# Scores of both softmax maps as alternating 64-row matmuls, drains on VectorE, and a head's Newton steps on GpSimd

## The chip, the core and the metric

The kernel runs on one core of a Trainium2 chip. The metric is the device time of one execution in microseconds (us). The engines of the core are TensorE (PE in the rows, its weight loads PEld), VectorE (DVE), ScalarE (ACT), GpSimd (POOL) and the DMA queue of SyncE (SP). Each works through its own list of instructions in order, and they wait for each other by semaphores.

## What is computed

One layer of a mixer: a projection feeds a differential attention (8 heads, two softmax maps per head) and a recurrent branch, and both go through one output projection. The part that the change touches is the attention with the output projection around it. Cut from the reference:

```python
def one_block(qblk):                                   # 128 queries
    s = jnp.einsum('bqhmd,bkhmd->bhmqk', qblk, k) * scale   # m: two maps, d = 64
    p = jax.nn.softmax(s, axis=-1)
    a = p[:, :, 0] - lam * p[:, :, 1]
    return jnp.einsum('bhqk,bkhe->bqhe', a, v)
o = diff_attention(q, k_all, v_all, lam)
att = (rms_norm(o, g_subln) * (1.0 - lam_init)) * jax.nn.silu(g_att)
...
out = jnp.concatenate([att, lru], axis=-1) @ w_out
x_new = x + gate * rms_norm(out, g_post)
```

There are 128 context and 1024 latent tokens. A block of context queries sees 128 keys, a block of latent queries 1152 (1024 latent and 128 cached).

## The kernel before, in words

To keep close to float32, every product is made of three matmuls: each operand is split into a high part in a rounded float32 and a low part that holds the rest, and high x high, high x low and low x high are added (`mm3`, L117 to L119).

Up to some 430 us the kernel normalises the input and works on the recurrent branch; from 430 to 730 us it projects queries, keys and values and stores them in DRAM (`qk_block`, `v_block`; per head `qs`, `ks`). Then comes the attention loop, up to some 1225 us, and after it the rest of the output projection and the final normalisation.

The loop has 72 tiles: 8 heads by 9 blocks of 128 queries. The block of context queries is a small tile of 128 keys; it stands first in each head but the last, and last in the last. `period(n)` emits the work of tile n, and the order of emission is the order on each engine. For a tile and a map:

- `scores(n, mp)` makes the scores in one of two PSUM buffers of three banks (tag `big`), 3 x 384 columns. Before, the high part of the query stands twice in its tile, in rows 0 to 63 and 64 to 127, and the key tile of a map holds the high and the low part of the keys one above the other. So one matmul of 128 rows (L1076) gives high x high and high x low at once, and one of 64 rows (L1078) adds low x high.
- VectorE takes the maximum (L1085) and corrects that of map 0 by a constant (L1088), ScalarE the exponential with its sum (L1092).
- `recip` and `combine` make the factor (L1100, L1102) and e1 x factor - e0 (L1111) of the tile before; ScalarE casts it to float16 (L1114), GpSimd makes the float16 remainder (L1115), and SP transposes both by DMA (L1117).
- `pv(n - 4)` multiplies the transposed weights of the tile four periods back with the values (27 matmuls of 128 columns), ScalarE copies the result to `ot` and squares it.

The buffers of the exponentials (`e0`, `e1`) and of the casts (`a16`) are two deep each.

Between these the loop does most of the output projection: a granule is three matmuls of 512 columns (`out_mm`), four granules fill a unit in the PSUM bank `po`, and a unit is drained into `acc` in SBUF (`out_evac`): the first 18 by a ScalarE copy, the next by a ScalarE copy to `ev` (L1039) and an add on GpSimd (L1040), the last few by VectorE (L1042). `GRANULES` lists for each period how many granules stand after map 0's scores and how many after map 1's.

When a head is done, `mean_squares` and `root` compute 1 / sqrt of its mean squares by Newton steps on 9 columns. Before, these wait in the list `tiny`, and `fill()` puts one behind each of the loop's VectorE instructions. Then `scale` multiplies the head's output on GpSimd (L1161), TensorE transposes it into the spare columns of score buffers (L1165), and VectorE multiplies in the gate (L1169).

## Time and profile before

| what | us |
|---|---|
| median of three runs (1293.74 to 1298.01) | 1294.49 |
| the profiled execution | 1297.48 |
| its span, first to last instruction | 1295.1 |
| TensorE / VectorE busy in the span | 1220.8 / 968.3 |
| ScalarE / GpSimd busy in the span | 680.1 / 479.1 |

How to read the rows below: a row of the timeline gives the start in the span, the length, the engine, the line, the operation and what it writes and reads; `x3` means three of one kind merged. Matmuls overlap in their pipeline, so the distance from one start to the next says what one costs, not its length. In brackets stands the idle time of the engine before the row and what ended it.

### The profile page before, as it was taken

How to read it: one execution, taken by the hardware profiler on the slowest of the kernel's cores; microseconds unless marked ns; L12 is line 12 of the kernel's file. 1: busy time of each engine (PE TensorE's matmuls, PEld its weight loads, DVE VectorE, ACT ScalarE, POOL GpSimd, SP SyncE). 2: the span in 40 equal slices, each digit the busy share in tenths (PEclk: the TensorE clock that was granted, in tenths of full speed). 3: DMA queues.
4: the chain of work that ended last, by engine and by line, in shares of the span. 5: the costliest groups of instructions: out<-in, count | busy, mean ns of one | idle time of the engine just before them, and what ended most of it. 6: DMA issues, size and time to landing. Idle time of an engine off the chain costs nothing.

```text
span 1295.1 us, 19733 instructions
## 1 busy us (share of the span) xinstructions
PE 1220.8 (94%) x7672; PEld 1069.4 (83%) x7672; DVE 968.3 (75%) x1253; ACT 680.1 (53%) x1152; POOL 479.1 (37%) x244
## 2 busy tenths in 40 slices
PE   6899999999999899999999699999999989999887
PEld 1499999999999899989999577776777766777666
DVE  4938779777979828666473257888898989899977
ACT  4446545654665233332232357677667676766632
POOL 0421112111212334424242214346655566555624
PEclk9999999999999899999999899999999998999999
DMA  9221222123212757446272659899899988899864
GB/s 364 103 72 41 91 93 93 60 74 111 76 54 102 214 165 220 151 161 167 88 218 68 228 127 201 193 214 249 174 214 224 226 218 191 201 207 217 205 202 167
DMA packets 262916, 208.62 MB, mean 161 GB/s; under 512 B 158876, under 2 KB 228252, under 8 KB 262056
## 3 DMA queue, kind: packets, MB, share of 16 engines
q1 hardware_dynamic: 262536, 206.52, 59.0%
q8 instruction: 60, 0.98, 0.3%
q10 hardware_dynamic: 288, 0.85, 0.2%
q14 instruction: 32, 0.26, 0.1%
HBM read 112.16 MB, written 56.90 MB: 131 GB/s over the span
## 4 chain that ended last, share of the span: by engine, by line
PE 67%; DVE 20%; issue 4%; DMA 4%; ACT 3%; SPq 1%; POOL 1%; DVEq 0%; ACTq 0%; POOLq 0%
PE s L1078 5%; DVE mx L1085 4%; PE s L1076 4%; PE po L117 3%; DVE e L1111 3%; PE ga L119 3%; PE ga L117 3%; PE ga L118 3%; PE po L119 3%; PE po L118 3%; PE v L118 2%; PE v L117 2%; PE v L119 2%; PE x L118 2%; PE x L119 2%
## 5 line engine op out<-in xcount | busy, mean ns | idle before, releaser
L114 POOL TENSOR_TENSOR wlo<-wraw,whi 128x1024 fp32r<-128x1024 f32 x48 | 129.5, 2698 | 421.6 <-ACT whi L262 418.0
L1115 POOL TENSOR_TENSOR a<-e,a 128x1152 f16<-128x1152 f32 (+1 forms) x72 | 156.0, 2166 | 212.3 <-ACT a L1114 210.3
L1085 DVE TENSOR_REDUCE mx<-s 128x1 f32<-128x1152 f32 (+1 forms) x144 | 176.8, 1233 | 65.8 <-PE s L1078 64.1
L1092 ACT ACTIVATE e<-s,mx 128x1152 f32<-128x1152 f32 (+1 forms) x144 | 162.4, 1128 | 77.0 <-DVE fa L1100 29.7
L1111 DVE SCALAR_TENSOR_TENSOR e<-e,fa,e 128x1152 f32<-128x1152 f32 (+1 forms) x72 | 119.0, 1653 | 6.7 <-DVE fa L1102 0.5
L1076 PE MATMUL s<-kt,qt 128*128 128x384 f32 (+1 forms) x400 | 100.3, 355 | 19.5 <-ACT e L1092 18.0
L117 PE MATMUL po<-woh,lt 128*128 128x512 f32 x216 | 97.2, 450 | 16.3 <-ACT e L1092 13.9
L1114 ACT CAST a<-e 128x1152 f16<-128x1152 f32 (+1 forms) x72 | 76.0, 1055 | 60.8 <-DVE e L1111 52.7
L1078 PE MATMUL s<-kt,qt 64*128 64x384 f32 (+1 forms) x400 | 107.0, 369 | 0.0
L117 PE MATMUL pv<-vt,t 128*128 128x128 f16 x584 | 103.5, 222 | 1.9 <-ACT ot L1130 1.9
L118 PE MATMUL pv<-vt,t 128*128 128x128 f16 x584 | 102.8, 220 | 0.0
L119 PE MATMUL pv<-vt,t 128*128 128x128 f16 x584 | 102.8, 220 | 0.0
L1076 PEld LDWEIGHTS s<-kt,qt 128*128 128x128 f32 x400 | 69.1, 192 | 31.8 <-ACT e L1092 24.3
L1078 PEld LDWEIGHTS s<-kt,qt 64*128 64x128 f32 x400 | 63.7, 187 | 34.8 <-issue 34.2
L119 PE MATMUL po<-woh,lt 128*128 128x512 f32 x216 | 86.7, 401 | 0.0
L118 PE MATMUL po<-wol,lt 128*128 128x512 f32 x216 | 86.6, 401 | 0.0
L117 PE MATMUL v<-whi,hTh 128*128 128x256 f32 x288 | 81.8, 284 | 0.0
L119 PE MATMUL v<-whi,hTl 128*128 128x256 f32 x288 | 81.5, 283 | 0.0
L118 PE MATMUL v<-wlo,hTh 128*128 128x256 f32 x288 | 81.5, 283 | 0.0
L117 PEld LDWEIGHTS po<-woh,lt 128*128 128x128 f32 x216 | 41.4, 192 | 41.1 <-issue 15.9
L117 PEld LDWEIGHTS <-t 128*128 128x128 f16 x584 | 57.5, 98 | 17.7 <-issue 17.5
L117 PE MATMUL k<-hTh,whi 128*128 128x384 f32 x192 | 66.4, 346 | 4.8 <-ACT qfk L633 4.8
(299 smaller groups left out, 3588.0 us busy)
## 6 DMA issues: line engine op xcount, KB each, us to landing
wraw<-in_w_in_dram SPq DMA_DIRECT2D x48, 512.0 KB, 3.5
qt<-qs SPq DMA_DIRECT2D x72, 192.0 KB, 3.6
lt<-mix SPq DMA_DIRECT2D x27, 512.0 KB, 4.6
kt<-ks SPq DMA_DIRECT2D x16, 640.0 KB, 6.2
qs<-hiq SPq DMA_DIRECT2D x32, 288.0 KB, 5.8
wa<-in_w_ada_dram SPq DMA_DIRECT2D x16, 512.0 KB, 10.9
wor<-in_w_out_dram SPq DMA_DIRECT2D x32, 256.0 KB, 3.3
mix<-amo SPq DMA_DIRECT2D x6, 1152.0 KB
```

Source lines behind the costliest of these rows:

```text
L114: eng.tensor_tensor(out=lo, in0=val, in1=f(hi), op=ALU.subtract)
L117: PE.matmul(out, lhsT=lh, rhs=rh, start=start, stop=False)
L118: PE.matmul(out, lhsT=lh, rhs=rl, start=False, stop=False)
L119: PE.matmul(out, lhsT=ll, rhs=rh, start=False, stop=stop)
L1076: PE.matmul(sps[:, j, :w_], lhsT=qt[:, mp], rhs=kt_[:, mp, c], start=True, stop=False)
L1078: PE.matmul(sps[:, j, :w_], lhsT=qt[rows, 2], rhs=kt_[rows, mp, c], start=False, stop=True)
L1085: V.tensor_reduce(out=d["mx"][:, mp:mp + 1], in_=sv, axis=AX.XY, op=ALU.max, negate=True)
L1092: S.activation(out=e_[:, :nk].rearrange("p (j c) -> p j c", c=w_), in_=sv, func=AF.Exp, bias=d["mx"][:, mp:mp + 1], accum_out=total)
L1111: V.scalar_tensor_tensor(out=e1, in0=e1, scalar=d["fa"], in1=e0, op0=ALU.mult, op1=ALU.subtract)
L1114: S.copy(out=a16[:, 0:nk], in_=e1)
L1115: G.tensor_tensor(out=a16[:, nk:2 * nk], in0=e1, in1=a16[:, 0:nk], op=ALU.subtract)
```

## The change

**Scores.** `scores(n)` now scores both maps of a tile in one go. The query is stored once, its high and low part as two tiles with map 0 in rows 0 to 63 and map 1 in rows 64 to 127, and so are the keys. Each of the three products is a matmul of 64 rows, and map 0 and map 1 take turns. On TensorE, before, around the second map of a tile (`s_1` is its score buffer, `kt` and `qt` keys and query, `po` the output projection):

```order
L119 MATMUL pv_8435<-vt_7449,t_25_8240 128x128
L1076 MATMUL s_1_8475<-kt_7925,qt_2_8185 128x384 [waits Activation_49]
L1076 MATMUL s_1_8475<-kt_7925,qt_2_8185 128x384 x2
L1078 MATMUL s_1_8475<-kt_7925,qt_2_8185 128x384 x3
L117 MATMUL po_1_1_8413<-woh_1_8094,lt_1_7776 128x512
```

and now, at a tile's start (`s_0` and `s_1` are the buffers of its two maps):

```order
L99 MATMUL po_0_1_8432<-wol_1_8283,lt_0_7761 128x512 [waits Pool_49]
L100 MATMUL po_0_1_8432<-woh_1_8282,lt_0_7761 128x512
L1038 MATMUL s_0_8535<-kt_8028,qt_2_8286 128x384 [waits DMAHW6_49,Activation_49]
L1038 MATMUL s_1_8536<-kt_8028,qt_2_8286 128x384 [waits Activation_49]
L1038 MATMUL s_0_8535<-kt_8028,qt_2_8286 128x384
```

Eighteen matmuls of two maps stand together, and the first two wait for one exponential each; value product and granules follow behind them, no longer between the maps.

**Softmax, drains and factor.** `softmax(n, mp)` holds what followed the scores. Both maxima of a tile come before the drain and the combination of the tile before. Every unit is drained by VectorE. The factor is a scalar instruction instead of a tensor one. On VectorE, before (maxima `mx`, factor `fa`, exponentials `e`):

```order
L1102 SCALAR_TENSOR_TENSOR fa_8466<-fa_8466,lam,kq_8269 128x1 [waits DVE_49]
L1111 SCALAR_TENSOR_TENSOR e_1_8411<-e_1_8411,fa_8466,e_0_8361 128x1152 [waits DVE_49,Pool_49]
L1085 TENSOR_REDUCE mx_8422<-s_1_8475 128x1 [waits PE_49]
L1085 TENSOR_REDUCE mx_8499<-s_0_8501 128x1 [waits PE_49]
L1088 TENSOR_SCALAR mx_8499<-mx_8499,lsig 128x1 [waits DVE_49]
L1100 RECIPROCAL fa_8543<-sm_8423 128x1 [waits Activation_49]
```

and now:

```order
L1050 TENSOR_REDUCE mx_8533<-s_0_8535 128x1 [waits PE_49]
L1053 TENSOR_SCALAR mx_8533<-mx_8533,lsig 128x1 [waits DVE_49]
L1050 TENSOR_REDUCE mx_8533<-s_1_8536 128x1 [waits PE_49]
L1004 TENSOR_TENSOR acc_6236<-acc_6236,po_1_1_8593 128x512 [waits PE_49]
L1067 RECIPROCAL fa_8607<-sm_8454 128x1 [waits Activation_49]
L1069 TENSOR_SCALAR fa_8607<-fa_8607,lam,kq_8381 128x1 [waits DVE_49]
L1077 SCALAR_TENSOR_TENSOR e_1_8480<-e_1_8480,fa_8607,e_0_8477 128x1152 [waits DVE_49,Pool_49]
```

The combination of the tile before moved from ahead of the second maximum to behind it, and a drain (L1004) stands between.

**Granules.** The list holds one number per period, 4 or 2 (8 in period 3); they stand behind `pv`.

**Newton steps.** `apart(h, 0)` puts four small instructions on GpSimd at the end of period b + 8 (b is the head's first period plus 4), `apart(h, 1)` two on VectorE and twelve on GpSimd at the end of b + 9, with `scale` behind them. This holds for seven heads; the last keeps its way. On GpSimd, before (`a` remainder of a tile, `acc` output sums, `ot` head output):

```order
L1115 TENSOR_TENSOR a_30_8614<-e_1_8560,a_30_8614 128x1152 [waits DMAHW1_49,Activation_49]
L1040 TENSOR_TENSOR acc_6280<-acc_6280,ev_0_8656 128x512 [waits Activation_49]
L1115 TENSOR_TENSOR a_31_8702<-e_1_8628,a_31_8702 128x1152 [waits DMAHW5_49,Activation_49]
L1161 TENSOR_TENSOR ot_7888<-ot_7888,y_7885 128x1152 [waits DVE_49]
L1115 TENSOR_TENSOR a_32_8779<-e_1_8716,a_32_8779 128x1152 [waits DMAHW0_49,Activation_49]
```

and now, up to the first of three equal rounds of four, and the end:

```order
L1121 TENSOR_TENSOR xc_7973<-xc_7973,tt_7972 128x9 [waits Pool_49]
L1081 TENSOR_TENSOR a_30_8754<-e_1_8648,a_30_8754 128x1152 [waits DMAHW7_49,Activation_49]
L1126 TENSOR_TENSOR tt_7972<-y_7971 128x9 [waits DVE_49,Pool_49]
L1127 TENSOR_TENSOR tt_7972<-tt_7972,xc_7973 128x9 [waits Pool_49]
L1128 TENSOR_SCALAR tt_7972<-tt_7972 128x9 [waits Pool_49]
L1129 TENSOR_TENSOR y_7971<-tt_7972,y_7971 128x9 [waits Pool_49]
...
L1146 TENSOR_TENSOR ot_7974<-ot_7974,y_7971 128x1152 [waits Pool_49]
L1081 TENSOR_TENSOR a_31_8858<-e_1_8730,a_31_8858 128x1152 [waits DMAHW3_49,Activation_49]
```

The adds of the output sums left GpSimd; the Newton steps stand between two remainders. The core of the diff:

```diff
-    qs = [dr.tile([P, 3, T], F32R, name=f"qs{h}") for h in range(NH)]
+    qs = [dr.tile([P, 2, T], F32R, name=f"qs{h}") for h in range(NH)]
...
             def send():
-                hi, lo = d["hl"]
-                if which == 0:
-                    for m2 in range(2):
-                        for r in (slice(0, 64), slice(64, 128)):
-                            move(out=qs[h][r, m2], in_=hi[64 * m2:64 * m2 + 64])
-                    move(out=qs[h][:, 2], in_=lo)
-                else:
-                    for mp in range(2):
-                        for part, val in enumerate((hi, lo)):
-                            r = 64 * (mp ^ part)
-                            move(out=ks[r:r + 64, mp, h, 0:T], in_=val[64 * mp:64 * mp + 64])
+                for part, val in enumerate(d["hl"]):
+                    move(out=ks[:, part, h, 0:T] if which else qs[h][:, part], in_=val)
...
             if first:
-                S.copy(out=dst, in_=po)
-            elif shared and turns["i"] % EVERY == 0:
-                ev = op.tile([P, 512], F32, tag="ev", name=f"ev{t}_{half}")
-                S.copy(out=ev, in_=po)
-                G.tensor_tensor(out=dst, in0=dst, in1=ev, op=ALU.add)
+                V.tensor_copy(out=dst, in_=po)
             else:
                 V.tensor_tensor(out=dst, in0=dst, in1=po, op=ALU.add)
...
-            for j, c in enumerate(cols):
-                PE.matmul(sps[:, j, :w_], lhsT=qt[:, mp], rhs=kt_[:, mp, c], start=True, stop=False)
-            for j, c in enumerate(cols):
-                PE.matmul(sps[:, j, :w_], lhsT=qt[rows, 2], rhs=kt_[rows, mp, c], start=False, stop=True)
...
+            for j in range(nk // w_):
+                c = slice(key0 + j * w_, key0 + (j + 1) * w_)
+                for x, (a, b) in enumerate(((0, 0), (0, 1), (1, 0))):
+                    for mp in range(2):
+                        rows = slice(64 * mp, 64 * mp + 64)
+                        PE.matmul(sps[mp][:, j, :w_], lhsT=qt[rows, a], rhs=kt_[rows, b, c], start=x == 0, stop=x == 2)
...
-            V.scalar_tensor_tensor(out=d["fa"], in0=d["fa"], scalar=lam, in1=kqs[h][:, i:i + 1], op0=ALU.mult,
-                                   op1=ALU.mult)
+            V.tensor_scalar(out=d["fa"], in0=d["fa"], scalar1=lam, scalar2=kqs[h][:, i:i + 1], op0=ALU.mult, op1=ALU.mult)
...
+        def apart(h, step):
+            d = heads[h]
+            kq, tt, xc, y = kqs[h], d["tt"], d["xc"], d["y"]
+            if step == 0:
+                G.tensor_tensor(out=tt, in0=kq, in1=kq, op=ALU.mult)
+                G.tensor_scalar(out=tt, in0=tt, scalar1=epsh[:, h:h + 1], scalar2=None, op0=ALU.mult)
+                G.tensor_scalar(out=xc, in0=xc, scalar1=-0.5 / P, scalar2=None, op0=ALU.mult)
+                G.tensor_tensor(out=xc, in0=xc, in1=tt, op=ALU.add)
+                return
+            for k in (1, 2):
+                newton(k, xc, y, tt)
+            for _ in range(3):
+                G.tensor_tensor(out=tt, in0=y, in1=y, op=ALU.mult)
+                G.tensor_tensor(out=tt, in0=tt, in1=xc, op=ALU.mult)
+                G.tensor_scalar(out=tt, in0=tt, scalar1=1.5, scalar2=None, op0=ALU.add)
+                G.tensor_tensor(out=y, in0=tt, in1=y, op=ALU.mult)
+            scale(h)
...
-            at_period(b + 8, lambda: mean_squares(h, 0, NT))
-            at_period(b + (9 if fast else 10), lambda: (fill(True), scale(h)))
+            at_period(b + 8, lambda: apart(h, 0))
+            at_period(b + 9, lambda: apart(h, 1))
...
-                scores(n, 0, lambda: granules(here[0]))
-            evac()
+                scores(n)
+                softmax(n, 0)
+                softmax(n, 1)
             m = n - LAG
             if 0 <= m < NTL:
                 pv(m)
+            granules(GRANULES.get(n, 0))
             if 0 <= n - 1 < NTL:
                 recip(n - 1)
                 combine(n - 1)
-            if n < NTL:
-                scores(n, 1)
-            granules(here[1])
```

## Rows read from the trace of the kernel before

**Rows 1.** The page: busy us, share of the span, instructions of each engine.
```profile
PE 1220.8 (94%) x7672; PEld 1069.4 (83%) x7672; DVE 968.3 (75%) x1253; ACT 680.1 (53%) x1152; POOL 479.1 (37%) x244
```
**Rows 2.** Windows: length, busy PE, PEld, DVE, ACT, POOL (instructions), clock, DMA.
```profile
430.00:730.00 300.00, 292.88 (x1925) 289.48 (x1925) 172.41 (x250) 91.68 (x180) 103.51 (x37) 0.98 0.56 167
800.00:1160.00 360.00, 341.44 (x2435) 260.38 (x2434) 313.15 (x421) 249.96 (x495) 200.83 (x110) 0.99 0.92 210
```
**Rows 3.** The same window for line 1088 alone: VectorE's busy time (instructions), clock, DMA.
```profile
800.00:1160.00 360.00, 11.44 (x54) 0.99 0.92 210
```
**Rows 4.** Timeline of TensorE in the projections: start, length, engine, line, operation, shapes.
```profile
721.76 0.33 PE L119 MATMUL ga<-hTh,wlo 128*128 128x384 f32 x1
721.93 0.33 PE L117 MATMUL ga<-hTh,whi 128*128 128x384 f32 x1
```
**Rows 5.** Timeline of TensorE in the loop: one map, a granule, a value product.
```profile
902.67 0.70 PE L1076 MATMUL s<-kt,qt 128*128 128x384 f32 x3
903.30 0.79 PE L1078 MATMUL s<-kt,qt 64*128 64x384 f32 x3
904.02 0.50 PE L117 MATMUL po<-woh,lt 128*128 128x512 f32 x1
904.36 0.39 PE L118 MATMUL po<-wol,lt 128*128 128x512 f32 x1
904.59 0.40 PE L119 MATMUL po<-woh,lt 128*128 128x512 f32 x1
904.83 0.23 PE L117 MATMUL pv<-vt,t 128*128 128x128 f16 x1
...
906.32 0.42 PE L1076 MATMUL s<-kt,qt 128*128 128x384 f32 x1
```
**Rows 6.** Waits from 730 to 1230 us: who waited for whom, us, times, longest.
```profile
PE s L1076 <- ACT e L1092: 18.0, 20, 2.4
```
**Rows 7.** Timeline of VectorE in an early tile.
```profile
758.11 1.36 DVE L1085 TENSOR_REDUCE mx<-s 128x1 f32<-128x1152 f32 x1 [2.08 <-PE s L1078]
...
759.63 0.15 DVE L1100 RECIPROCAL fa<-sm 128x1 f32<-128x1 f32 x1
...
760.08 1.42 DVE L1111 SCALAR_TENSOR_TENSOR e<-e,fa,e 128x1152 f32<-128x1152 f32 x1
```
**Rows 8.** Timeline of ScalarE in that tile, and of a handoff to TensorE.
```profile
759.81 1.23 ACT L1092 ACTIVATE e<-s,mx 128x1152 f32<-128x1152 f32 x1 [1.96 <-DVE fa L1100]
...
888.47 1.22 ACT L1092 ACTIVATE e<-s,mx 128x1152 f32<-128x1152 f32 x1 [0.25 <-DVE tt L170]
889.59 0.19 ACT L1092 ACTIVATION_READ_ACCUMULATOR e<-s,mx 128x1 f32 x1
...
889.84 0.44 PE L1076 MATMUL s<-kt,qt 128*128 128x384 f32 x1 [0.98 <-ACT e L1092]
```
**Rows 9.** Line 1042 in the loop: durations in ns, minimum, median, maximum.
```profile
L1042 DVE TENSOR_TENSOR acc<-acc,po x2: 674/676/678, 1216.7 to 1222.8; 128x512 f32<-128x512 f32 x2
```
**Rows 10.** Groups of instructions: busy us, mean ns of one, idle before.
```profile
L1115 POOL TENSOR_TENSOR a<-e,a 128x1152 f16<-128x1152 f32 x64 | 152.5, 2384 | 195.3 <-ACT a L1114 195.0
L1114 ACT CAST a<-e 128x1152 f16<-128x1152 f32 x64 | 73.6, 1150 | 50.2 <-DVE e L1111 44.5 <-DMA t<-a 5.6
L1102 DVE SCALAR_TENSOR_TENSOR fa<-fa,lam,kq 128x1 f32<-128x1 f32 x72 | 45.2, 628 | 2.1
L1161 POOL TENSOR_TENSOR ot<-ot,y 128x1152 f32<-128x1152 f32 x7 | 15.9, 2274 | 5.1 <-DVE y L174 5.1
...
L1115 POOL TENSOR_TENSOR a<-e,a 128x128 f16<-128x128 f32 x8 | 3.4, 428 | 17.1 <-ACT a L1114 15.3 <-issue 1.7
L503 POOL MEMSET xp<- 128x6 f32 x2 | 0.2, 104 | 0.0
```
**Rows 11.** Timeline of two weight loads in the map of rows 5.
```profile
903.30 0.18 PEld L1078 LDWEIGHTS s<-kt,qt 64*128 64x128 f32 x1 [0.26 <-issue]
903.40 0.19 PEld L1078 LDWEIGHTS s<-kt,qt 64*128 64x128 f32 x1
```

More of the change, by code (lines that the diff above doesn't have):

```diff
@@ L755, in send @@
             def send():
-                for mp in range(2):
-                    for part in range(2):
-                        r = 64 * (mp ^ part)
-                        move(out=ks[r:r + 64, mp, :, T:],
-                             in_=cks[part][64 * mp:64 * mp + 64].rearrange("p (h c) -> p h c", h=NH))
+                for part in range(2):
+                    move(out=ks[:, part, :, T:], in_=cks[part].rearrange("p (h c) -> p h c", h=NH))
             after(2 + 1, send)
```

101 lines of the change are left out of this document (34 added, 67 removed).

## The prediction

> **What bounds the kernel now.** The page first [rows 1]: TensorE is busy 94% of the span, VectorE 75%. By stage [rows 2], TensorE is full from 430 to 730 us (292.9 of 300) and in the attention loop (341.4 of 360), where VectorE comes second (313.2) and the DMA engines are at 0.92; the granted clock is 0.98 and 0.99, so nearly always at 2.4 GHz. The diff changes the loop, and a tile of the loop is what I price. The window of 360 us holds 54 first-map corrections, one per tile [rows 3]: 360 / 54 = 6.67 us per tile, six of the 54 being small tiles of 128 keys.
>
> Inside a tile TensorE is the queue that hardly empties. A 384-column matmul starts 0.173 us after the one before [rows 4]. One map is three matmuls of 128 rows and three of 64: 902.67 to 903.30, on to 904.02, and the next matmul then takes 0.34 instead of 0.23 us [rows 5]. Six times 0.173 is 1.04; what is over (0.11 + 0.20 + 0.11 = 0.42 us) goes to changing from 128 to 64 rows and back. A tile's scores are 2 x (1.04 + 0.42) = 2.92 us. The value product takes 1.49 (904.83 to 906.32), a granule 3 x 0.23 = 0.69, and 124 granules on 45 tiles make 1.91 per tile. Sum 6.32; the rest of the 6.67 is transposes and waits, of which the exponential's are 18 us in all [rows 6].
>
> **The change, part by part.**
>
> *Scores.* Twelve matmuls become eighteen of 64 rows that alternate between the two halves of the array, and one change of rows per tile goes, 0.42 us. What a pair from two halves costs no row shows. Bounds: 0.175 us, if both stream side by side with their loads hidden, and 0.35 us, one after the other. I take 0.175, the nearest row: three 64-row matmuls behind each other already hide their loads (903.30 to 904.02 is 3 x 0.173 and the change) [rows 5], and the two halves share neither array rows nor PSUM banks. A tile's scores are then 9 x 0.175 + 0.42 = 2.00 instead of 2.92, and 0.92 us of TensorE per tile comes free.
>
> The Trainium skill (TensorEngine Tiling (Array Packing), Key Properties) says that different tiles of the array can run weight loads and matmuls in parallel. By the Trainium skill the pair would be 0.175 too; no run here shows it.
>
> *The order, which takes most of that back.* Before, map 0 of the next tile was scored while map 1 was still being exponentiated. Now the two maps need both PSUM buffers of the tile before, and since they alternate, all matmuls but the first wait for the second exponential. That closes a loop. Set 0 at the start of a tile's first maximum. The exponential of map 0 starts at 1.70 (758.11 to 759.81); the second maximum runs from 1.52 (758.11 to 759.63) to 2.88; the exponential of map 1 starts at 2.98 (an estimated 0.10 of handoff, which is what 1.70 holds behind maximum and correction) and is read out 1.31 later (888.47 to 889.59, and 0.19), at 4.29; TensorE starts 0.06 behind it, at 4.35 [rows 7, 8]. Map 0 has seven pair steps left, 7 x 0.175 = 1.23, then 0.34 for its last matmul and 0.04 to the maximum: **5.96 us** for a tile with two granules. TensorE idles some 1.3 us in it; the 20 waits of this kind before were 0.9 each with the clock at 0.99 [rows 2, 6], so I charge nothing for the clock.
>
> *Drains move from ScalarE and GpSimd to VectorE*, ahead of the reciprocal. In a tile with four granules TensorE ends them at 1.55 + 11 x 0.23 + 0.40 = 4.49; the add takes 0.68 [rows 9], reciprocal and factor 0.45, the combination 1.42 [rows 7], less 0.08 of overlap: VectorE reaches the next maximum at **6.92 us**. The tile behind pays as well: its second exponential writes a buffer that GpSimd must have read. Combination done at 7.0, cast 1.15, GpSimd's remainder 2.38 [rows 10], handoffs 0.11: 10.64, which is 3.72 in the following tile; with a handoff 3.77 instead of 2.98, so that tile takes 5.96 + 0.79 = **6.75 us**. What ScalarE and GpSimd lose (a copy and an add for each of 34 units) was off the path.
>
> *The factor* becomes a scalar instruction like the correction, 11.44 / 54 = 0.21 us [rows 3]; before, it took 0.63 on average [rows 10]. My tile times hold 0.21 already, so no second credit.
>
> *Sum over tiles.* Of tiles 4 to 48, 17 have four granules, each followed by one at 6.75: (17 x 6.92 + 17 x 6.75 + 11 x 5.96) / 45 = 6.62. A small tile is bound by TensorE: 1.55 + 1.91 + 2.00 = 5.46. Mean (8 x 6.62 + 5.46) / 9 = 6.49 against 6.67, and 0.18 x 72 = **-13 us**.
>
> *Newton steps.* Thirteen small VectorE instructions per head leave; VectorE doesn't set the loop in most tiles, so no credit. GpSimd gets 4 and then 12 dependent ones on 9 columns, and the scaling of 2.1 (2.27 on average) behind them, for 7 heads. No row has such an operation: below it stands a memset at 0.10, above it the same kind of subtraction on 128 columns at 0.43 [rows 10]. I take 0.2, nearer the memset, because 9 columns are. 12 x 0.2 + 2.1 = 4.5 us behind a remainder that ended at 3.72 is 8.2; the next cast is ready near 6.2, so that remainder is 2.0 late, of which about 1.2 is slack: 0.8 x 7 = **+6 us**.
>
> *Stores and loads.* A tile's query goes from 192 to 128 KB, 4.7 MB less in all; stores of a q head go from five to two, of a k head from four to two. Loads are issued three tiles ahead, and the stores run under a full TensorE (430 to 730 us) [rows 2], so nothing is counted; without that cover, 64 KB at the loop's 210 GB/s are 0.3 us per tile.
>
> The profiled execution took 1297.5 us, its span 1295.1; the median is 1294.5, 3.0 lower, and -13 + 6 = -7 us holds for either. **Forecast 1287.5 us.**
>
> **Rivals.**
>
> *Loads set the pace.* Two 64-row loads start 0.10 us apart (903.30, 903.40) with nothing between them, and each takes 0.18 to 0.19 [rows 11]. If the loads of both halves go through one path, at 0.10 to 0.11 each, a pair costs up to 0.22. Two-granule tiles take 6.26, those behind four granules 7.05, small ones 5.85; mean 6.70, which is +2 us, and with the Newton term +8: **1303 us**. Against it: wherever a row has a stream longer than its load, the load is hidden.
>
> The Trainium skill (TensorE: Matmul & The Clock Gate, LDWEIGHTS) has a load's time follow its columns and not its rows, 128 / 1.2 = 107 ns. The trace agrees, since the loads of 64 rows are no shorter than 0.18 us [rows 11]. By the Trainium skill eighteen loads are an estimated 1.9 us, more than nine pairs of 0.175.
>
> *It doesn't do what it says.* If the halves don't overlap, scores are 18 x 0.175 + 0.42 = 3.57 us. Tiles with four granules are then bound by TensorE, 3.57 + 1.49 + 2.77 = 7.83, the others by the loop, 7.18; mean 7.43, small ones 7.0; over all 7.38, +51 us: **1346 us**.
>
> *GpSimd becomes the bound (slower).* Its place is the buffer of the second exponential, once per head. Each 0.1 us on a small instruction adds 12 x 0.1 x 7 = 8 us; from 0.29 us on the gain of 13 is gone, and at 0.43 the time is 1287.5 + 19 = **1307 us**. For it: each of the twelve waits for the one before. Against it: 9 columns.
>
> **Chances.** Forecast 0.46, loads 0.22, no overlap 0.17, GpSimd 0.15. About 0.3% (4 us) is what a measurement of this kernel can tell from no change. Faster 0.44 (0.40 from the forecast, 0.02 each from loads and GpSimd), within it 0.18 (0.06, 0.08, 0.04), slower 0.38 (0.12 from loads, 0.17, 0.09). The forecast's own range is 1272 (half of the followers don't pay their 0.79, which is 10 us, and the Newton steps lie in slack, 6) to 1295 (0.29 us per Newton instruction). The range 1272 to 1340 adds the loads, GpSimd and the lower part of no overlap; it leaves out the rest of that and a tail below.
>
> **What would show it.** Right: the score matmuls of one tile start 0.17 to 0.18 us apart per pair, a tile's scores take 2.0 us, TensorE idles ahead of the second score matmul with the second exponential as releaser, and tiles follow each other at 6.0, 6.8 and 6.9 us by their granules. Wrong: pairs at 0.22 or 0.35; GpSimd instructions on 9 columns above 0.3 us; a second exponential that waits for GpSimd by several us at each head; longer TensorE idles followed by a granted clock at 1.2 GHz.

## The result, and the profile after

The changed kernel takes **1345.6 us** (median of 4 runs, 1341.4 to 1348.9) where the kernel before takes 1294.8 in the same session: a ratio of 1.0386, interval 1.035 to 1.0423. It is 51 us slower; the forecast was 7 us faster, and the time lies above the range. The profiled execution's span is 1347.2 us.

The page of the changed kernel, which answers to [rows 1] (busy us, share of the span, instructions of each engine):

```profile
PE 1201.7 (89%) x8072; PEld 1074.1 (80%) x8072; DVE 940.0 (70%) x1228; ACT 653.4 (48%) x1100; POOL 467.3 (35%) x322
```

The two windows of [rows 2] (length, busy PE, PEld, DVE, ACT, POOL with instructions, granted clock, DMA share, GB/s):

```profile
430.00:730.00 300.00, 292.86 (x1925) 289.47 (x1925) 176.50 (x251) 91.60 (x180) 102.34 (x37) 0.98 0.42 149
...
800.00:1160.00 360.00, 297.53 (x2552) 241.22 (x2550) 262.20 (x365) 214.18 (x427) 177.93 (x157) 0.95 0.80 184
```

And VectorE's correction alone, line 1053 now, in the loop's window, as in [rows 3]:

```profile
800.00:1160.00 360.00, 10.73 (x50) 0.95 0.80 184
```

The projections (430 to 730) are untouched. In the loop's window every engine is busy for less time than before: TensorE 297.5 us instead of 341.4, VectorE 262 instead of 313, GpSimd 178 instead of 201. 50 tiles fit instead of 54, so a tile takes 7.2 us instead of 6.67. A stretch in which nobody is busier and everything is slower has a chain of waits in it; the waits of the loop (730 to 1270 us: who for whom, us, times, longest) name it:

```profile
ACT a L1080 <- DVE e L1077: 79.6, 49, 5.0
ACT e L1059 <- DVE mx L1053: 77.8, 57, 8.3
PE s L1038 <- ACT e L1059: 71.7, 64, 4.5
DVE mx L1050 <- PE s L1038: 53.1, 39, 4.2
DVE acc L1004 <- PE po L100: 43.4, 33, 5.3
ACT e L1059 <- POOL a L1081: 39.6, 34, 3.7
DVE acc L1002 <- PE po L100: 38.7, 18, 17.5
```

TensorE waits 71.7 us for the exponential where it waited 18.0 [rows 6]. Two kinds are new: the exponential waits for GpSimd's remainder (39.6 us; the kernel before shows none), and VectorE waits for the output product in the drains (82.1 us in 51 waits). One of the 51, 17.5 us at the loop's start, is no loss: the kernel before has a wait of 18.0 us at the same place, in the maximum.

First the step that came out as forecast. TensorE in the changed kernel (start, length, engine, line, operation, shapes):

```profile
952.57 0.39 PE L100 MATMUL po<-woh,lt 128*128 128x512 f32 x1
952.88 1.85 PE L1038 MATMUL s<-kt,qt 64*128 64x384 f32 x18
954.66 0.23 PE L98 MATMUL pv<-vt,t 128*128 128x128 f16 x1
...
952.88 1.53 PEld L1038 LDWEIGHTS s<-kt,qt 64*128 64x128 f32 x18 [0.36 <-ACT ot L1096]
```

Eighteen 64-row matmuls take 1.85 us from first start to last end. The last of them starts 1.51 us behind the first, which is eight steps from pair to pair (0.17 to 0.19 each, the first 0.28), and its own length of 0.34 makes up the rest. So the two halves stream side by side.

Then how long a tile takes, from the first maximum of one tile to that of the next. The table is worked out from the starts of the 72 first maxima in each trace: medians of tiles 9 to 48 by kind, in us. "Newton" are the two tiles of each head in which the effect of its Newton steps shows (the seventh and eighth). The two right columns are experiments that follow.

| kind of tile | forecast | changed | drain behind | and three buffers |
|---|---|---|---|---|
| two granules, behind two | 5.96 | 6.06 | 6.05 | 6.05 |
| two granules, behind four | 6.75 | 6.11 | 6.03 | 6.05 |
| four granules, behind two | 6.92 | 7.12 | 6.37 | 6.39 |
| small (128 keys) | 5.46 | 7.05 | 5.41 | 5.24 |
| Newton | about 7.0 | 8.42 | 7.74 | 6.59 |

And by stage, from the same starts, in us:

| kernel | tiles 0 to 9 | 9 to 63 | 63 to 71 | from the last tile's first maximum to the end |
|---|---|---|---|---|
| before | 69.9 | 358.1 | 61.9 | 72.8 |
| changed | 76.1 | 388.2 | 67.7 | 81.4 |
| changed, Newton steps back | 76.2 | 380.5 | 66.9 | 80.4 |
| changed, three buffers | 73.8 | 368.7 | 65.8 | 81.3 |
| changed, drain behind | 74.4 | 361.8 | 62.5 | 77.6 |
| drain behind, three buffers | 75.2 | 354.2 | 62.5 | 76.4 |
| the same, last transposes late | 74.7 | 352.4 | 63.4 | 74.4 |
| before, Newton steps on GpSimd | 70.0 | 351.4 | 61.6 | 72.8 |

Each row is one profiled execution. For "drain behind, three buffers" and "the same, last transposes late" it was the slowest of ten, 7.2 and 5.4 us above the median, so small differences between rows say little.

### The profile page after: what moved, and what is told of

Its sections match the earlier page's. It is cut to its first block, busy times and chain, and to the rows that moved or that the text cites. A ratio compares the mean times of both kernels' runs of the same rounds, so it can differ in the third digit from the quotient of the medians.

```text
span 1347.2 us, 20474 instructions
## 1 busy us (share of the span) xinstructions
PE 1201.7 (89%) x8072; PEld 1074.1 (80%) x8072; DVE 940.0 (70%) x1228; ACT 653.4 (48%) x1100; POOL 467.3 (35%) x322
## 4 chain that ended last, share of the span: by engine, by line
PE 55%; DVE 14%; issue 11%; POOL 9%; ACT 5%; DMA 5%; SPq 0%; DVEq 0%; POOLq 0%; ACTq 0%
POOL a L1081 5%; PE s L1038 4%; PE ga L99 3%; PE ga L98 3%; PE ga L100 3%; PE v L100 3%; PE v L99 3%; PE v L98 3%; PE x L99 2%; PE x L100 2%; PE x L98 2%; PE g L98 2%; PE g L99 2%; PE g L100 2%; PE k L98 2%
## 5 line engine op out<-in xcount | busy, mean ns | idle before, releaser
L1059 ACT ACTIVATE e<-s,mx 128x1152 f32<-128x1152 f32 (+1 forms) x144 | 162.2, 1127 | 135.7 <-DVE mx L1053 77.8
L1038 PE MATMUL s<-kt,qt 64*128 64x384 f32 (+1 forms) x1200 | 157.3, 371 | 77.4 <-ACT e L1059 71.7
L1038 PEld LDWEIGHTS s<-kt,qt 64*128 64x128 f32 x1200 | 121.1, 201 | 117.8 <-ACT e L1059 98.5
L1077 DVE SCALAR_TENSOR_TENSOR e<-e,fa,e 128x1152 f32<-128x1152 f32 (+1 forms) x72 | 112.3, 1559 | 7.0 <-DVE fa L1069 0.5
L98 PE MATMUL pv<-vt,t 128*128 128x128 f16 x584 | 111.4, 231 | 3.6 <-ACT ot L1096 3.4
L99 PE MATMUL pv<-vt,t 128*128 128x128 f16 x584 | 110.8, 230 | 0.0
L100 PE MATMUL pv<-vt,t 128*128 128x128 f16 x584 | 110.4, 229 | 0.0
L98 PE MATMUL po<-woh,lt 128*128 128x512 f32 x216 | 93.0, 430 | 14.5 <-DMA lt<-mix 13.7
L100 PE MATMUL po<-woh,lt 128*128 128x512 f32 x216 | 86.3, 399 | 0.0
L98 PEld LDWEIGHTS <-t 128*128 128x128 f16 x584 | 60.6, 104 | 13.7 <-issue 12.5
L98 PE MATMUL x<-hTh,whi 128*128 128x384 f32 x192 | 65.5, 341 | 2.3 <-DVE hTh L377 2.3
L99 PE MATMUL x<-hTl,whi 128*128 128x384 f32 x192 | 65.7, 342 | 1.7 <-DVE hTl L95 1.0
L99 PE MATMUL k<-hTl,whi 128*128 128x384 f32 x192 | 66.0, 344 | 0.0
## 6 DMA issues: line engine op xcount, KB each, us to landing
wa<-in_w_ada_dram SPq DMA_DIRECT2D x16, 512.0 KB, 11.4
```

The source lines that it names most:

```text
L98: PE.matmul(out, lhsT=lh, rhs=rh, start=start, stop=False)
L99: PE.matmul(out, lhsT=lh, rhs=rl, start=False, stop=False)
L100: PE.matmul(out, lhsT=ll, rhs=rh, start=False, stop=stop)
L1038: PE.matmul(sps[mp][:, j, :w_], lhsT=qt[rows, a], rhs=kt_[rows, b, c], start=x == 0, stop=x == 2)
L1059: S.activation(out=e_[:, :nk].rearrange("p (j c) -> p j c", c=w_), in_=sv, func=AF.Exp, bias=d["mx"][:, mp:mp + 1], accum_out=total)
L1077: V.scalar_tensor_tensor(out=e1, in0=e1, scalar=d["fa"], in1=e0, op0=ALU.mult, op1=ALU.subtract)
```

## The experiments

All are compared with the kernel before on the same chip; the time is a median.

### Are the Newton steps on GpSimd the cause?

The trace of the changed kernel suggests it. GpSimd, then ScalarE's exponentials, then VectorE, around one head's steps:

```profile
908.68 0.20 POOL L1126 TENSOR_TENSOR tt<-y 128x9 f32<-128x9 f32 x1
908.96 0.21 POOL L1127 TENSOR_TENSOR tt<-tt,xc 128x9 f32<-128x9 f32 x1
...
910.45 1.29 POOL L1128 TENSOR_SCALAR tt<-tt 128x9 f32<-128x9 f32 x1
...
913.29 2.11 POOL L1146 TENSOR_TENSOR ot<-ot,y 128x1152 f32<-128x1152 f32 x1
915.36 2.36 POOL L1081 TENSOR_TENSOR a<-e,a 128x1152 f16<-128x1152 f32 x1
...
914.00 1.22 ACT L1059 ACTIVATE e<-s,mx 128x1152 f32<-128x1152 f32 x1
...
917.76 1.22 ACT L1059 ACTIVATE e<-s,mx 128x1152 f32<-128x1152 f32 x1 [2.45 <-POOL a L1081]
...
910.22 1.42 DVE L1077 SCALAR_TENSOR_TENSOR e<-e,fa,e 128x1152 f32<-128x1152 f32 x1
...
915.51 3.43 DVE L1077 SCALAR_TENSOR_TENSOR e<-e,fa,e 128x1152 f32<-128x1152 f32 x1
922.09 1.36 DVE L1050 TENSOR_REDUCE mx<-s 128x1 f32<-128x1152 f32 x1 [3.16 <-PE s L1038]
```

Twelve small instructions from 908.68 on, the scale, and only at 915.36 the remainder, for which the second exponential waits 2.45 us; this tile takes 9.9 us (912.15 to 922.09). Ahead of the twelve GpSimd also splits output weights here (1.29 us from 907.43), but that is not the cause: four of the six heads of tiles 9 to 62 have no split at this place, and their tiles take 8.1 to 10.4 us. Two runs asked whether the move is what costs 51 us.

**The changed kernel with the steps back on VectorE:**

```
-            at_period(b + 8, lambda: apart(h, 0))
-            at_period(b + 9, lambda: apart(h, 1))
+            at_period(b + 8, lambda: mean_squares(h, 0, NT))
+            at_period(b + (9 if fast else 10), lambda: (fill(True), scale(h)))
```

> The changed kernel with the heads' Newton steps back on VectorE, scattered between its other work, and the scale back at its old periods; pair scores, drains on VectorE and the single store stay. Theory A (the chain of twelve small dependent instructions and the scale on GpSimd stands ahead of the remainder that frees the second exponential's buffer, once per head, and the idle TensorE then loses its clock): the two tiles that follow a head's Newton steps fall from 9.8 and 7.8 us to below 7.5, a head from 64.7 to some 60 us, and the kernel from 1345.6 to 1312 us (1300 to 1322). Theory B (the loop itself: both score buffers wait for both exponentials, VectorE also drains, and the clock falls in the idle times wherever they are): the time hardly moves, 1336 to 1350.

1338.7 us, ratio 1.0328 (1.0298 to 1.0359): 7 us come back of the 34 expected, which is theory B's range, and theory A falls. The slow tiles didn't go, they moved two tiles ahead, where the two of a head take 16.3 us together in the mean instead of 17.7. There, on VectorE, GpSimd and ScalarE:

```profile
897.99 2.18 DVE L1135 SCALAR_TENSOR_TENSOR tt<-kq,epsh 128x9 f32<-128x9 f32 x1
...
897.75 2.40 POOL L1081 TENSOR_TENSOR a<-e,a 128x1152 f16<-128x1152 f32 x1 [3.49 <-ACT a L1080]
...
900.39 1.22 ACT L1059 ACTIVATE e<-s,mx 128x1152 f32<-128x1152 f32 x1 [2.20 <-DVE mx L1053]
```

The first Newton instruction has 9 columns and takes 2.18 us: it ends when GpSimd's remainder ends, and the first exponential waits behind it. On VectorE the steps are hardly cheaper.

**The kernel before with the steps on GpSimd** (the same two lines the other way round, and `apart` added):

> The kernel before with the one edit that its heads' Newton steps go to GpSimd as the changed kernel has them (means in the eighth period after the head's first, the steps and the scale in the ninth); scores, drains and stores stay as before. Theory A: the chain costs much the same there, 3 to 5 us a head: 1294.8 becomes 1318 (1310 to 1330). Theory B (the chain hurts only where the pair loop has no slack): 1292 to 1302.

1292.1 us, ratio **0.9956 (0.9942 to 0.9971)**: 5.6 us faster than the kernel before, where theory A wanted 23 slower. GpSimd issues the same chain there, and all waits of exponentials for it are one of 0.6 us:

```profile
ACT e L1092 <- POOL a L1115: 0.6, 1, 0.6
```

So the move itself is good, and something else in the changed kernel makes it hurt.

### Is the second exponential's buffer the way in?

```
-            e_ = kb.tile([P, KEYS], F32, tag=f"e{mp}", name=f"e{n}_{mp}", bufs=2)
+            e_ = kb.tile([P, KEYS], F32, tag=f"e{mp}", name=f"e{n}_{mp}", bufs=2 + mp)
```

(The tiles of the last stage that share this buffer get the same count.)

> The changed kernel with three buffers instead of two for the second map's exponentials; nothing else. The wait of the second exponential for GpSimd's remainder (39.6 us in 34 waits between 725 and 1280) has to go. Theory A: GpSimd reaches the tiles' chain through this buffer, so most of what it costs comes back, less what the combination's and the transposed transfer's lateness still costs: 1325 us (1312 to 1335). Theory B: the wait covers another one that is next in line (first exponential, drains, or GpSimd holding VectorE's port): 1338 to 1350.

1322.2 us, ratio 1.0199 (1.0173 to 1.0225), 23.4 us less, inside theory A's range. The wait for GpSimd is gone from the exponential's group, and the wait for the maximum has become a little shorter, not longer (63.7 us, 77.8 in the changed kernel; busy, mean ns, idle before and what ended it):

```profile
L1059 ACT ACTIVATE e<-s,mx 128x1152 f32<-128x1152 f32 (+1 forms) x144 | 162.0, 1126 | 85.6 <-DVE mx L1053 63.7 <-DVE sga L1154 17.6 <-DVE fa L1067 2.3
```

So this is a way in. The two Newton tiles of a head fall from 17.7 to 14.5 us together (means of the six heads in tiles 9 to 62). But the tile with four granules stays at 7.12 and the small tile at 7.15 (medians): what holds those two is not this buffer. Why had the kernel before never waited there, with the same two buffers? Medians of tiles 11 to 57, worked out from the traces:

| us | before | changed | combination first | drain behind |
|---|---|---|---|---|
| from the second exponential's end to the combination | 2.3 | 7.6 | 0.7 | 5.2 |
| from the remainder's end to the exponential that needs its buffer | 4.4 | 0.0 | 6.0 | 0.6 |

Before, the combination stood between the two maxima of the next tile, early. In the changed kernel it stands behind both of them and behind the drain. In the median 4.4 us of slack went to nothing (it is under 0.1 us in 25 of the 47 tiles, in the kernel before never under 2.6), and where a queue has no slack a delay on GpSimd is a delay of the tile. This is theory C of the next runs.

### What makes the combination late?

**Factor and combination of the tile before at the head of the period:**

```
             run(early.get(n, []))
+            if 0 <= n - 1 < NTL:
+                recip(n - 1)
+                combine(n - 1)
...
             granules(GRANULES.get(n, 0))
-            if 0 <= n - 1 < NTL:
-                recip(n - 1)
-                combine(n - 1)
```

> The changed kernel with the factor and the combination of the tile before placed at the head of a period, before this tile's two maxima on VectorE (and so their copy before this tile's exponentials on ScalarE); the drains stay last, the Newton steps stay on GpSimd. Theory C (in the changed kernel the combination stands behind both maxima and the drain, starts 7.6 us after its second exponential ended instead of 2.3, and so the remainder ends 0.0 us before the exponential two tiles on wants its buffer instead of 4.4): this slack comes back, GpSimd's Newton chain fits into it, the waits of the second exponential for GpSimd (39.6 us) go, a head falls from 64.7 to 58 to 60 us; 1313 us (1300 to 1325). Theory D (the loop is slow because TensorE idles behind both exponentials and loses its clock, whatever the order on VectorE): 1335 to 1350.

1312.1 us, ratio 1.0121 (1.0095 to 1.0148), as theory C had it, with the Newton steps still on GpSimd. The waits of the exponentials for GpSimd are gone from the list (730 to 1270 us); a head takes 61.2 us in the mean, a little more than the 58 to 60 expected.

**The drain behind the combination**, both still behind the maxima:

```
+            if 0 <= n - 1 < NTL:
+                recip(n - 1)
+                combine(n - 1)
             granules(GRANULES.get(n, 0))
-            if 0 <= n - 1 < NTL:
-                recip(n - 1)
-                combine(n - 1)
```

> The changed kernel with one swap: the drain of the output product stands behind the factor and the combination on VectorE instead of ahead of them, and the two maxima stay ahead; nothing else. VectorE stood 84 us in the drains' waits for TensorE's product. Theory C1 (it is this wait ahead of the combination that makes it late): most of the slack comes back, 1322 us (1312 to 1335). Theory C2 (the two maxima ahead of it do it, or the drains only move their wait before the next tile's maximum): 1336 to 1350.

**1308.4 us**, ratio 1.0086 (1.0066 to 1.0107): the swap of two neighbours on one engine gives back 37 of the 51 us, more than either theory allowed (1312 at the lowest). But not in the way that theory C1 had it. Little of the slack comes back, 0.6 us in the median, and the exponential still waits for GpSimd; what goes is VectorE's wait in the drain (43.4 us before the swap). The waits from 730 to 1270 us with the swap:

```profile
ACT e L1059 <- POOL a L1081: 25.8, 13, 5.4
DVE acc L1004 <- PE po L100: 5.7, 5, 2.1
```

VectorE in a tile with four granules, in the changed kernel:

```profile
948.38 1.36 DVE L1050 TENSOR_REDUCE mx<-s 128x1 f32<-128x1152 f32 x1 [0.68 <-PE s L1038]
...
949.90 1.35 DVE L1050 TENSOR_REDUCE mx<-s 128x1 f32<-128x1152 f32 x1
952.99 0.69 DVE L1004 TENSOR_TENSOR acc<-acc,po 128x512 f32<-128x512 f32 x1 [1.74 <-PE po L100]
953.60 0.16 DVE L1067 RECIPROCAL fa<-sm 128x1 f32<-128x1 f32 x1
...
954.17 1.42 DVE L1077 SCALAR_TENSOR_TENSOR e<-e,fa,e 128x1152 f32<-128x1152 f32 x1
955.50 1.35 DVE L1050 TENSOR_REDUCE mx<-s 128x1 f32<-128x1152 f32 x1
```

and with the swap, in another tile with four granules:

```profile
1001.54 1.36 DVE L1050 TENSOR_REDUCE mx<-s 128x1 f32<-128x1152 f32 x1 [1.02 <-PE s L1038]
...
1003.06 1.35 DVE L1050 TENSOR_REDUCE mx<-s 128x1 f32<-128x1152 f32 x1
1004.33 0.15 DVE L1067 RECIPROCAL fa<-sm 128x1 f32<-128x1 f32 x1
...
1004.89 1.42 DVE L1077 SCALAR_TENSOR_TENSOR e<-e,fa,e 128x1152 f32<-128x1152 f32 x1
1006.23 0.68 DVE L1004 TENSOR_TENSOR acc<-acc,po 128x512 f32<-128x512 f32 x1
1007.79 1.36 DVE L1050 TENSOR_REDUCE mx<-s 128x1 f32<-128x1152 f32 x1 [0.88 <-PE s L1038]
```

In the first, VectorE stands idle for TensorE's product for 1.74 us while the factor, whose inputs have long been there, queues behind; the next tile's maximum starts without a wait, right behind the combination: VectorE is late, and the tile takes 7.12 us (948.38 to 955.50). In the second the factor starts with the end of the maximum, the drain finds its product done, and VectorE is early by 0.88 us: 6.25 us (1001.54 to 1007.79). The tile table shows it for all: four granules 7.12 to 6.37 (the tile shown first, 29, takes 6.39 with the swap), small tiles 7.05 to 5.41. The two Newton tiles of a head hardly change, 17.7 to 17.4 us together in the mean. So the change has two ways to cost time, and each run takes away another: the swap frees VectorE, which was late at the next maximum, and the third buffer frees the Newton tiles from GpSimd's queue.

**The drains back on ScalarE and GpSimd**, at their new place:

```
-                V.tensor_copy(out=dst, in_=po)
+                S.copy(out=dst, in_=po)
...
-                V.tensor_tensor(out=dst, in0=dst, in1=po, op=ALU.add)
+                ev = op.tile([P, 512], F32, tag="ev", name=f"ev{t}_{half}")
+                S.copy(out=ev, in_=po)
+                G.tensor_tensor(out=dst, in0=dst, in1=ev, op=ALU.add)
```

> The changed kernel with the drains back as they were: ScalarE copies the product out of the banks and GpSimd adds it; they stay at their new place in the period, the Newton steps stay on GpSimd. Theory C (what counts is how late the combination and the remainder come): VectorE no longer waits for the product, but ScalarE does, ahead of the copy for the remainder, and GpSimd gets one addition of some 0.9 us more in most tiles ahead of the remainder: no gain or a loss, 1340 to 1365. Rival (VectorE's load by the drains is the cause): 1318 to 1332.

1330.2 us, ratio 1.0256 (1.0233 to 1.0278): theory C's number was wrong, and the rival's held. The ordinary tiles come down to 6.0 to 6.4 as with the swap, since nothing stands ahead of the combination on VectorE; the Newton tile goes up, to 11.4 on average, since GpSimd's queue is longer by the additions (1.35 us each in the mean, where 0.9 was expected). VectorE's load is still not the cause: the swap leaves all the drains on VectorE and gains more than twice as much.

### What is left

The drain behind the combination, and three buffers on top:

> The changed kernel with the drain behind the combination (as in the run before, 1308.4 us) and three instead of two buffers for the second map's exponentials; Newton steps on GpSimd. Theory C (GpSimd's queue reaches the tiles' chain through that buffer; 25.8 us in 13 waits are left of it, all at the Newton and scale tiles, where two tiles take 9.9 and 7.5 us): those tiles fall to some 7 us, the kernel to 1294 (1286 to 1301). Rival (the Newton tiles lose by VectorE's combination sharing its port with GpSimd, 3.35 instead of 1.42 us, whatever the buffers): 1303 to 1310.

1297.3 us, ratio **1.0000 (0.9976 to 1.0023)**, inside theory C's range. The Newton tiles come down to 6.6 in the median, the kernel is level with the one before. Not all of it is gain: of the 3.2 us that a head's two Newton tiles lose in the mean, 2.4 return in the two tiles behind them. In this trace TensorE waits 9.1 us, in four waits, for the keys of the next head, where the kernel before and the swap alone have no such wait; no run loaded the keys earlier.

The drain behind the combination, and the Newton steps back on VectorE:

> The changed kernel with the drain behind the combination and the Newton steps back on VectorE, two buffers. Theory C (with the drain out of the way a slack of 0.6 us is left, which the chain of twelve small steps on GpSimd overruns once a head and the scale alone overruns less): 1299 us (1292 to 1305), where moving the steps back alone gained 7. Rival (the steps cost VectorE as much as GpSimd, as in the kernel before, where moving them gained 5.6): 1306 to 1314.

1303.5 us, ratio 1.0063 (1.0042 to 1.0085), inside theory C's range.

All three:

> The changed kernel with the drain behind the combination, three buffers for the second map's exponentials and the Newton steps back on VectorE. Theory C: no Newton tile is left and the scale fits into the slack; 1288 us (1280 to 1295), which would be faster than the kernel before by some 8. Rival (what remains over the kernel before lies at the loop's start, at the transposes and in the tail, some 12 us): 1295 to 1303.

1304.5 us, ratio 1.0061 (1.0035 to 1.0088): 7 us more than with the steps left on GpSimd, and above both ranges, theory C's (1280 to 1295) and the rival's. So the price of the same move is -5.6 us in the kernel before, +7 in the changed one, +5 with the drain behind, and -7 once the buffer has slack as well (differences of medians). The first and the last are clear of noise; for the two in the middle the intervals of the ratios overlap.

Combination first, with the output product ahead of the value product on TensorE, so that its drain is ready early; and the same with three buffers:

```
+            granules(GRANULES.get(n, 0))
             if 0 <= m < NTL:
                 pv(m)
-            granules(GRANULES.get(n, 0))
```

> The changed kernel with factor and combination at the head of the period (1312.1 us alone) and the output product issued ahead of the value product on TensorE, so that its drain is ready earlier and no longer stands ahead of the next factor. Theory C: with the combination early and no drain in its way a tile takes 6.2 us throughout, 1302 us (1294 to 1308). Rival (what is left there is the Newton tiles and the transposes, which this does not touch): 1308 to 1315.

> The changed kernel with factor and combination at the head of the period, the output product ahead of the value product (1301.7 us so far), and three buffers for the second map's exponentials. Theory: with the early combination the buffer is free 5.5 us before it is wanted, so a third one brings nothing: 1299 to 1303. Rival (at the Newton tiles the queue of GpSimd still overruns 5.5 us): 1290 to 1298.

1301.7 us, ratio 1.0046 (1.003 to 1.0062), and 1299.7 us, ratio 1.0011 (0.9997 to 1.0025). Where the remainder ends 5.5 us before its buffer is wanted, a third buffer brings next to nothing.

### What is alternating worth?

```
-            for j in range(nk // w_):
-                c = slice(key0 + j * w_, key0 + (j + 1) * w_)
-                for x, (a, b) in enumerate(((0, 0), (0, 1), (1, 0))):
-                    for mp in range(2):
+            for mp in range(2):
+                rows = slice(64 * mp, 64 * mp + 64)
+                for j in range(nk // w_):
+                    c = slice(key0 + j * w_, key0 + (j + 1) * w_)
+                    for x, (a, b) in enumerate(((0, 0), (0, 1), (1, 0))):
```

In the changed kernel:

> The changed kernel with the same 64-row score matmuls in another order, all nine of the first map and then all nine of the second, so that two halves of the array lie beside each other only where the maps meet; nothing else. The score work grows from 1.85 to some 3.1 us a tile. Theory A (Newton chain): the tiles behind the Newton steps stay at 9 to 10 us, the others are held by TensorE at 6.7 to 7: 1345 to 1375 us. Theory B (alternating ties both score buffers to both exponentials, where the first map alone could start after the first): the lost 1.3 us of TensorE's idle time is filled and the clock stays up: 1315 to 1335. If two 64-row matmuls in fact do not lie beside each other at all, the time is that of the changed kernel, 1343 to 1349, and the score rows do not lengthen.

1353.2 us, ratio 1.0431 (1.0404 to 1.0458), 7.6 more (the intervals just overlap). The time lies in the range of theory A, whose mechanism the Newton steps on VectorE had already refuted; theory B's gain did not come. With the drain behind the combination:

> The changed kernel with the drain behind the combination (1308.4 us) and its 64-row score matmuls map by map instead of alternating; nothing else. In the changed kernel as it was this cost only 7.6 us, with 1.25 us of TensorE work more in each of 72 tiles. Theory E (the late combination hid what alternating is worth; with it out of the way TensorE's work counts again): 1330 us (1322 to 1345). Theory F (a tile is bound by the chain maximum, two exponentials, next scores, in which the first map's scores alone could stand earlier, so that alternating brings next to nothing): 1305 to 1316.

1321.4 us, ratio 1.0185 (1.0157 to 1.0214), 13.0 more: just below theory E's interval and above F's. The rows tell why it lies between (TensorE, map by map):

```profile
816.51 2.83 PE L1038 MATMUL s<-kt,qt 64*128 64x384 f32 x18
822.33 2.87 PE L1038 MATMUL s<-kt,qt 64*128 64x384 f32 x18
```

The scores take 2.83 us instead of 1.85, yet these tiles with two granules follow each other in 5.83 us, less than the 6.05 of alternating: only the first map's matmuls need the first exponential's buffer, and the second map's come later. (In the changed kernel, map by map took TensorE's wait for the exponential from 53.8 to 13.4 us in the loop's window.) With four granules, behind two, a tile takes 7.02 instead of 6.37 (medians as in the table), and a head's two Newton tiles 18.7 together instead of 17.4 in the mean. So alternating gains where TensorE is the bound or the chain is disturbed, and loses 0.2 us in the plain tile.

### The tail

In the changed kernel TensorE stands before the last tile's transposes, with products queued behind them:

```profile
1266.33 1.06 PE L1150 MATMUL s<-ident,ot 128*128 128x128 f32 x3 [7.71 <-ACT ot L1205]
```

These transposes were issued in the scores of the second map, behind the value product; they now stand ahead of it. Put back for the last tile alone:

```
...
+            if late(n) and n < NTL:          # late(n): n == NTL - 1
+                turns(n, 0)
+                turns(n, 1)
```

> The changed kernel with the transposes of the very last tile (and their read-out) issued behind its value and output products, as the kernel before has them, and nothing else. The trace shows TensorE standing 7.7 us there, with 1.9 us of products queued behind, for the scaled outputs from ScalarE. Theory: the stretch from the last maximum to the end falls from 81.4 towards 73 us, but the products that now fill the wait were only part of it: 1340 us (1336 to 1343). Rival: the last head's own chain (combination, copy, transposed transfer, values) ends later than the transposes anyway: 1343 to 1349.

> The changed kernel with the drain behind the combination, three buffers for the second map's exponentials (1297.3 us so far) and the last tile's transposes behind its value and output products. Theory: what is left over the kernel before is in the tail, where TensorE stands before these transposes; 1294 us (1290 to 1297). Rival (the tail hangs on the last head's chain, not on these products): 1297 to 1300.

1342.5 us, ratio 1.0347 (1.0324 to 1.037), 3 less than the changed kernel; on the best order 1293.7 us, ratio **0.9972 (0.9954 to 0.999)**, 3.6 less. Both times lie in the ranges of the theory, but the intervals overlap with those of the kernels without the edit; the stretch at the end is 3.4 and 2.0 us shorter in the traces. The second is the changed kernel with three corrections, 0.3% faster than the kernel before. The kernel before with nothing but the Newton steps moved (0.9956) has the lowest median of all that ran, though its interval overlaps with this one.

## Why the prediction was wrong, point by point

- **Pairs at 0.175 us: right.** 1.85 us for a tile's scores against 2.00. The rival without overlap gave 1346 us, which is the time that came out, and its mechanism is refuted by the row of eighteen matmuls in 1.85 us. A time that fits says nothing of a cause. The Trainium skill (TensorEngine Tiling (Array Packing), Key Properties) has different tiles of the array load and stream in parallel; the trace agrees, with 1.53 us of busy loads for eighteen. The rival of loads that set the pace is refuted by the same row.
- **The closed loop, 5.96 us: right**, 6.05 measured. This step held a warning that wasn't drawn: by the prediction's own figures TensorE's work was 6.32 us in the mean tile and the loop closes at 5.96, so of the 0.92 us of TensorE that come free some 0.36 could be gained.
- **The drain: seen, and sized wrong.** The prediction let VectorE reach the next maximum at 6.92 in a tile with four granules (7.12 measured) and charged 0.79 to the tile behind. Behind the tile shown above the second exponential does wait 0.76 us for GpSimd, and that tile takes 6.85; in the median of such tiles it is only 6.11. So the cost of a drain in a four-granule tile was in the sum: of the 26 us that the swap gave back in tiles 9 to 62, 16 came from tiles with four granules and their followers, whose price the forecast had charged. (The terms of the 6.92 add up to 6.96. And two tiles with two granules each also end a unit: 14 of the 45 tiles have such a drain, which the sum doesn't price, and four of the 17 followers have four granules themselves. These hardly matter: two granules behind two take 6.06.) What it missed is the small tile, "bound by TensorE: 5.46". Its median is 7.05. In three of the six small tiles of the loop VectorE comes to the next maximum late, without a wait (7.05, 6.06 and 8.57 us); with the drain behind the combination in none, and the median is 5.41.
- **Newton steps, +0.8 us a head: the term that failed.** The two Newton tiles take 17.7 us together in the mean (9.84 and 7.83), 3.6 us a head more than their forecast with the 0.8 in it. Set against the forecast by kind of tile, tiles 9 to 62 take 32 us too long: 22 in the twelve Newton tiles, 8 in the six small ones, and 2 in the other 36. Two errors. The instruction: 0.2 us taken, 0.29 from start to start measured (908.68, 908.96), and 1.29 where VectorE's combination runs beside it. The slack: "about 1.2 is slack", where the trace shows 0.0 in the median; with a third buffer the two tiles take 14.5 us, near their forecast of 14.0. The rival named the place exactly, the second exponential's buffer once per head, but its price per 0.1 us of instruction counted no neighbour. And it is not a price of the move alone: the same move gains 5.6 us in the kernel before.
- **The clock, charged nothing: wrong, its own price not isolated.** Behind an idle stretch of the Newton tile above TensorE runs at 1.2 GHz:

```profile
912.10:918.40 6.30, 3.57 (x36) 2.70 (x34) 6.07 (x6) 3.53 (x5) 5.97 (x7) 1.00 1.00 227
918.40:925.20 6.80, 6.08 (x41) 5.58 (x42) 3.61 (x5) 4.10 (x9) 5.28 (x3) 0.50 0.90 216
```

  TensorE was busy 3.57 of 6.30 us at a granted clock of 1.00 (2.4 GHz), and then ran 6.8 us at 0.50; seventeen score matmuls took 3.24 us there, and 1.83 at 757.93, where the granted clock was 1.00. Over the loop's window the clock is 0.95 instead of 0.99. The swap of the drain gave back 37 us with the clock still at 0.95, so the clock is not where the bulk went; no run took it away alone.
- **No credit for VectorE's Newton instructions: wrong.** In the kernel before, one of these steps (9 columns, 3 in the last head) has a mean of 0.67 us in the heads, though its median is 0.17 and its longest 2.25, and 0.17 in the stage ahead of the loop (group, busy us, mean ns, idle before):

```profile
L172 DVE TENSOR_TENSOR tt<-tt,xc 128x9 f32<-128x9 f32 (+1 forms) x30 | 20.2, 673 | 0.7
...
L172 DVE TENSOR_TENSOR tc<-tc,xc 128x9 f32<-128x9 f32 x3 | 0.5, 170 | 0.1
```

  The rows were there to be read. That they are why the move gains in the kernel before is likely, but no run shows it by itself.
- **Start, last head and tail, priced at 0.18 us a tile like the rest: wrong.** Against the kernel before, the start (tiles 0 to 9) loses 6.2 us, tiles 63 to 71 lose 5.8, and the stretch behind them 8.6. Of the tail 2 to 3 us are the transposes moved ahead of the products. In the best order the start still loses 4.8 us, the last head 1.5 and the tail 1.6. The start's cause was not tried and stays open; the trace only says where it is: tile 3, whose period issues eight granules in both kernels, and tile 4 behind it take 17.6 us together instead of 13.6, and 19.1 in the best order.
- **The factor, the stores and the loads**: little of the difference points to them; the projections' window is the same to 0.02 us of TensorE's time, and TensorE's waits for keys and queries in the loop are 4.8 us in three waits, against 1.1 in one before. None of the three was tried by itself.

In short: the forecast of the loop was reached (tiles 9 to 63 in 352.4 us, 6.53 a tile against the 6.49 of the sum) only after the combination had been moved ahead of the drain, a third buffer added and the transposes put back. What lost the time against the kernel before is first the order on VectorE: an instruction that waits for TensorE stands ahead of one that is ready and on whose result GpSimd, ScalarE and with them the next tiles depend. It makes VectorE late (37 us with the swap), and together with the maxima ahead of the combination it takes the slack that GpSimd's Newton steps needed (23 us with the third buffer; the two overlap, 48 us together). What the forecast failed on is the second: the slack that it counted on for the Newton steps was not there.

## What to carry to other kernels

Before a step is moved to an in-order queue, work out how long before its deadline each of that queue's results is ready, in every kind of tile; where it is zero, even a small addition can delay the tile, and where it was 4 us the same addition was a gain. Put what waits for another engine behind what is ready: the swap of two neighbouring statements was worth 37 us here, five times what undoing the suspected change was. And freeing an engine gains only up to the next bound: alternating takes 0.98 us of TensorE off a tile's scores and was worth 13 us in 72 tiles, 0.18 a tile. Look what the loop is closed by before counting the engine's saving.

## What the runs showed of the hardware

VectorE's operations on two tensors and GpSimd's instructions hold each other up, in both directions, until the other's instruction ends. A 9-column step on VectorE took 2.18 us beside a remainder on GpSimd (0.22 at its shortest), a 9-column step on GpSimd took 1.29 us beside VectorE's combination (0.20 to 0.26 alone), and the combination took 3.43 instead of 1.42 beside a remainder. It holds for the whole loop of the changed kernel: the 42 combinations of full tiles that began with no GpSimd instruction under way took 1.42 to 1.45 us each, the 22 that began beside one up to 3.46. The maximum, which reads one tensor, took 1.36 us at most in all 144 cases of the kernel before. The Trainium skill (SBUF — State Buffer, SBUF: two separate sides) describes the pair of ports that the two engines share as a lock which one of them holds for a whole instruction while the other is blocked; the trace agrees, since 2.18 us is the remainder's 2.40 from 897.75 on less what had passed of it at 897.99. By that rule a short step's price is set by what the other engine happens to run, which is why a mean from another stage told nothing here.
